# Moving the output matrices of a state-space layer behind the last attention scores

## The chip, the cores and the metric

The kernel runs on one core of a Trainium2 chip. The metric is the time of one execution on the device, in microseconds; the profile is of one such execution. The engines have separate instruction queues: TensorE (PE, with its weight loads as PEld), VectorE (DVE), ScalarE (ACT), GpSimd (POOL) and SyncE (SP), which here issues all large DMA transfers. Each works its queue in order and waits at semaphores for the others.

## What is computed

One layer of a streaming encoder over 256 frames and 16 meta tokens, width 1024: differential attention and a state-space model (S5) beside each other, an output projection, a layer norm, and a mixture of 32 experts with 4 of them for each token. Cut to what matters:

```
proj = h @ w_in                       # q, k, v (4 heads, 2 maps of 64), u (512 columns)
p = softmax(q k^T / 8 + bias)         # two maps for each head, chunk-causal
w = p[map 0] - lam * p[map 1]
att = rms_norm(w @ v)
x = scan(Abar, Bbar u);  y = Re(C x) + d * u;  ssm = glu(gelu(y))
h = layer_norm(alpha * h + [att | ssm] @ w_out)
h = layer_norm(alpha * h + moe(h))    # 32 experts, three 1024 x 1024 matrices each
```

## The kernel before

The program is written with a manual schedule: each engine's instructions run in the order of the program text. The first stage handles norm, projections, scores, states and output projection; the second streams the weights of the 32 experts through a ring of 19 chunks of 1 MB in SBUF (`ring`, `chunk`, `load_to`, issued by SP at line 551) and multiplies each with the tokens that chose it (line 1204). A chunk's place in the ring is also the place of earlier tensors: of the state tables `eb` (slot 6), the projection weights, and the matrices `AB` (slot 4), so the first chunks are issued as those are released.

The state-space model is computed in blocks of four frames. `AB` first holds the input matrices; they are transposed on TensorE into `BAT` (lines 472 to 481; odd groups are copied from PSUM by VectorE, even ones by ScalarE). `output_matrices(ri)`, for the real and the imaginary part, then makes the output matrices: `products` are three VectorE instructions over 128 x 1024 (lines 382 to 387, with `pw` as scratch), and `between_zeros` two ScalarE copies into `AB` (line 392).

Between them run four rounds, one for each head h. `states_a` are 8 products on TensorE, `states_b` nine VectorE instructions with two scans (lines 594 to 606). `scores_a(h, i)` takes the score products of the two maps in query block i (line 617), adds the bias and finds the maximum on VectorE (line 622), and takes Exp with a row sum on ScalarE (line 626). `scores_b(h, i)` inverts the sums (line 631), multiplies the second by lambda (632), scales the second map by it (633) and combines both maps (636), all on VectorE. `output_matrices(0)` stands inside round 0 between `scores_a` and `scores_b`, `output_matrices(1)` inside round 1. The k projections go to `kT` through a ScalarE copy (lines 652, 659, 667), one round ahead. `values(h)` projects v (copied by ScalarE at line 641), `value_rows(h)` transposes it (line 647, copies at 648 and 649); those of heads 0 and 1 lie in rounds 2 and 3.

After the last scores stand the lag products (lines 704 and 708), 128 small products that read both parts of `AB`; `values(2)`; `lag_b`, which copies their result (`KS`, line 719), adds the diagonal (720) and fills `ML` by eight VectorE and eight ScalarE copies (726, 728); `values(3)`; the loads of the second half of `w_out` and of the router's and bias rows; `split_w(1)`, which splits four pieces of `w_out` into a high part on ScalarE (570) and a low part on VectorE (572); `value_rows(2)` and `value_rows(3)`. Then follow the attention products (`av_a`, lines 763 to 781), the outputs of the state-space model (`out_a`, 811 and 813), the output projection (`mix`, 866 to 868), the norm, the router, and the first expert.

Of the kernel before, what the change touches and what calls it, by code (L numbers as in the profile page):

```python
# [15 lines left out]
AF = mybir.ActivationFunctionType  # L16
OP = mybir.AluOpType
# [47 lines left out]
def hybrid_layer(ctx, tc, I, out):  # L65
    nc = tc.nc
    V, S, G, T, SP = nc.vector, nc.scalar, nc.gpsimd, nc.tensor, nc.sync
# [9 lines left out]
    def nb(n=1):  # L77
        b = bank[0]
        if b + n > 8:
            b = 0  # L80
        bank[0] = (b + n) % 8
        return b

    def slot(i, shape, name, dt=F32):
        return per.tile(shape, dt, name=name, tag=f"slot{i}")
# [11 lines left out]
    def lw(shape, name, dt=F32, tag=None, bufs=None):  # L97
        return low.tile(shape, dt, name=name, tag=tag or name, bufs=bufs)
# [10 lines left out]
    def pt(shape, name, dt=F32, tag=None, bufs=None):  # L109
        return pool.tile(shape, dt, name=name, tag=tag or name, bufs=bufs)  # L110
# [74 lines left out]
    AB = slot(4, [128, 2, 16, 4, 2, 16], "AB")  # L185
# [87 lines left out]
    for db in range(8):  # L273
        if db % 2:
            S.activation(hT[:, db, :], PS[:, hb[db], :NP], AF.Identity, bias=VC[:, 8 + db:9 + db],
                         scale=VC[:, db:db + 1])
        else:
            V.tensor_scalar(hT[:, db, :], PS[:, hb[db], :NP], VC[:, db:db + 1], VC[:, 8 + db:9 + db],
                            op0=OP.mult, op1=OP.add)
# [62 lines left out]
    FW = pt([128, 2, 4, 16], "FW")  # L342
# [32 lines left out]
    def products(ri, src, tab, op, ta, tb):  # L375
        def sv(j):
            return src[:, j][:, :, None, :].to_broadcast([128, 16, 4, 16])

        def tv(j):
            return tab[:, j].rearrange("p t a -> p a t")[:, :, :, None].to_broadcast([128, 16, 4, 16])  # L380

        V.tensor_tensor(ta, sv(0), tv(ri), op=OP.mult)
        V.tensor_tensor(tb, sv(1), tv(1 - ri), op=OP.mult)
        if op == "r":
            V.tensor_tensor(ta, tb, ta, op=OP.subtract)
        else:
            V.tensor_tensor(ta, ta, tb, op=OP.add if op == "+" else OP.subtract)

    def between_zeros(dst, ri, src):
        for g2 in range(2):  # L390
            h = slice(64 * g2, 64 * g2 + 64)
            S.activation(dst[h, ri, :, :, g2], src[h], AF.Copy)

    pwf = lw([128, 1024], "pw", tag="vr")
    pw = pwf.rearrange("p (a t c) -> p a t c", a=16, t=4)
# [36 lines left out]
    CC = s8b[:, 0:512].rearrange("p (r a c) -> p r a c", r=2, a=16)  # L432
    for ri in range(2):
# [4 lines left out]
        for g2 in range(2):  # L438
            h = slice(64 * g2, 64 * g2 + 64)
            srcv = PS[h, b].rearrange("p (a g c) -> p a g c", a=16, g=2)[:, :, g2]  # L440
# [7 lines left out]
    def proj(name, fb, n0):  # L448
        b = nb()
        for kb in range(8):  # L450
            T.matmul(PS[:, b, :NP - n0], WIN[name][kb][:, fb * 128:(fb + 1) * 128], hT[:, kb, n0:],
                     start=(kb == 0), stop=(kb == 7))
        return PS[:, b, :NP - n0]
# [16 lines left out]
    BAT = [slot(f"5{c}", [128, 16, 128], "BAT") for c in "ab"]  # L470
    for ri in range(2):
        for a in range(4):
            b = nb()
            for j in range(4):
                T.transpose(PS[:, b, j * 128:(j + 1) * 128],
                            AB[:, ri, 4 * a + j].rearrange("p t g c -> p (t g c)"), ident)
            srcv = PS[:, b].rearrange("p (j c) -> p j c", j=4)
            if a % 2:
                V.tensor_copy(BAT[ri][:, 4 * a:4 * a + 4], srcv)
            else:  # L480
                S.activation(BAT[ri][:, 4 * a:4 * a + 4], srcv, AF.Copy)


    sl0 = slot("0a", [128, 2, D], "sl0")
# [3 lines left out]
    tmc = [sl0[:, j].rearrange("p (a t c) -> p a t c", a=16, t=4) for j in range(2)]  # L488

    def output_matrices(ri):  # L490
        products(ri, CC, FW, "+r"[ri], tmc[ri], pw)
        between_zeros(AB, ri, tmc[ri])

    MG = slot(1, [128, 2, 2048], "MG")
    load(MG[:, 1, :], "w_glu", 0, [[512, 128], [128 * 512, 4], [1, 512]])
# [62 lines left out]
    def load_to(n):  # L558
        while nload[0] < min(n, len(stream)):
            chunk(nload[0])  # L560
            nload[0] += 1
# [4 lines left out]
    def split_w(j, s_, l_, ks):  # L566
        if j not in W_HI:
            W_HI[j], W_LO[j] = parts4(s_, "wh", FR), parts4(l_, "wl", FR)
        for k in ks:
            S.activation(W_HI[j][k], W_OUT[j][k], AF.Copy)  # L570
        for k in ks:
            V.tensor_sub(W_LO[j][k], W_OUT[j][k], W_HI[j][k].bitcast(F32))
# [4 lines left out]
    def states_a(fb):  # L577
        vb = nb(2)
        for ri in range(2):
            for j in range(4):  # L580
                P = 4 * fb + j
                T.matmul(PS[:, vb + ri, j * 68:(j + 1) * 68], BAT[ri][:, P], u4[:, P, :], start=True, stop=True)
        VB[fb] = PS[:, vb:vb + 2, :272]
# [29 lines left out]
    def scores_a(h, i):  # L613
        nk, j0 = (144, 128) if i == 0 else (272, 0)
        sb = nb(2)
        for m in range(2):
            T.matmul(PS[:, sb + m, :nk], qT[64 * m:64 * m + 64, h, i * 128:(i + 1) * 128],
                     kT[64 * m:64 * m + 64, h, :nk], start=True, stop=True)
        s_ = sc2[:, (2 * h + i) % 2]
        mx, nm, sm_, r_ = (pt([128, 2], f"a{j}", bufs=2) for j in range(4))  # L620
        for m in range(2):
            V.tensor_tensor_reduce(s_[:, m, :nk], PS[:, sb + m, :nk], Tz[:, h, j0:j0 + nk], 1.0, -3e38,
                                   op0=OP.add, op1=OP.max, accum_out=mx[:, m:m + 1])
        V.tensor_scalar(nm, mx, -1.0, None, op0=OP.mult)
        for m in range(2):
            S.activation(s_[:, m, :nk], s_[:, m, :nk], AF.Exp, bias=nm[:, m:m + 1], accum_out=sm_[:, m:m + 1])
        SC[h, i] = s_, sm_, r_, nk

    def scores_b(h, i):
        s_, sm_, r_, nk = SC[h, i]  # L630
        V.reciprocal(r_, sm_)
        V.tensor_mul(r_[:, 1:2], r_[:, 1:2], lam)
        V.tensor_scalar(s_[:, 1, :nk], s_[:, 1, :nk], r_[:, 1:2], None, op0=OP.mult)
        w = aw[i][:, h]
        PW[h, i] = w
        V.scalar_tensor_tensor(w[:, :nk], s_[:, 0, :nk], r_[:, 0:1], s_[:, 1, :nk], op0=OP.mult, op1=OP.subtract)


    def values(h):
        vT = lw([128, NP], "vT", bufs=2)  # L640
        S.activation(vT, proj("v", h, 0), AF.Copy)
        return vT

    def value_rows(h, vT):
        b = nb()
        for blk, n in ((0, 128), (1, 128), (2, 16)):
            T.transpose(PS[:n, b, blk * 128:blk * 128 + 128], vT[:, blk * 128:blk * 128 + n], ident)
        S.activation(vr[:, 0:2, h * 128:(h + 1) * 128], PS[:, b, 0:256].rearrange("p (a e) -> p a e", a=2), AF.Copy)
        S.activation(vr[:16, 2, h * 128:(h + 1) * 128], PS[:16, b, 256:384], AF.Copy)
# [3 lines left out]
    states_b(0)  # L653
    scores_a(0, 0)
    scores_a(0, 1)
    output_matrices(0)
    states_a(1)
    scores_b(0, 0)
    S.activation(kT[:, 2, :], proj("k", 2, 0), AF.Copy)
    scores_b(0, 1)  # L660
    states_b(1)
    scores_a(1, 0)
    scores_a(1, 1)
    output_matrices(1)
    states_a(2)
    scores_b(1, 0)
    S.activation(kT[:, 3, :], proj("k", 3, 0), AF.Copy)
    scores_b(1, 1)
    states_b(2)
    vr = lw([128, 3, 512], "vr")  # L670
    vt0 = values(0)
# [12 lines left out]
    vt1 = values(1)  # L684
# [10 lines left out]
    def lt_(shape, name, tag=None, bufs=None):  # L695
        return lpool.tile(shape, F32, name=name, tag=tag or name, bufs=bufs)

    kb_ = nb()
    for fb in range(4):
        for j in range(4):  # L700
# [16 lines left out]
    def lag_b():  # L717
        KS = lt_([128, 4, 128], "KS", tag="y0")
        S.activation(KS, PS[:, kb_].rearrange("p (f c) -> p f c", f=4), AF.Copy)
        V.tensor_add(KS[:, :, 0:32], KS[:, :, 0:32], Dm)  # L720
        for j in range(4):
            for t in range(4):
                dst = ML[32 * t:32 * t + 32, :, j, 32 * t:128]
                srcv = KS[32 * j:32 * j + 32, :, 0:128 - 32 * t]
                if t < 2:
                    V.tensor_copy(dst, srcv)
                else:
                    S.activation(dst, srcv, AF.Copy)

    vt0 = values(2)  # L730
    lag_b()
    load_to(3)
    vt1 = values(3)
    wo0 = slot(3, [128, 4, D], "wo0")
    W_OUT[0] = [wo0[:, k] for k in range(4)]
    load(wo0, "w_out", 0, [[D, 128], [128 * D, 4], [1, D]])
# [6 lines left out]
    for j, n in enumerate(("b_gate", "b_up", "b_down")):  # L743
        load(bf[32 * j:32 * j + 32], n, 0, [[D, 32], [1, D]])
    split_w(1, 5, 0, (0, 1, 2, 3))
    value_rows(2, vt0)
    value_rows(3, vt1)
    load_to(5)


# [457 lines left out]
    def in_place(t, w):  # L1208
        return lambda kb: CH[place[t, w, kb // 2]][:, kb % 2]
# [227 lines left out]
    t, g, o, _, m = UNITS[u_]  # L1437
# [8 lines left out]
    def do_jobs(n):  # L1446
        for _ in range(n):
            f, *x_ = jobs.pop(0)
            f(*x_)

    r_ = linear(SI[t], 2, in_place(t, 2), transposed(ACT.pop(u_), m), m, {0: lambda: do_jobs(2), 2: lambda: do_jobs(2), 4: lambda: do_jobs(1), 6: lambda: do_jobs(1)})
# [100 lines left out]
```

## Time and profile before

| | |
|---|---|
| median of 3 runs | 1146.16 us (1142.4 to 1146.54) |
| profiled execution | 1143.38 us |
| its span, first to last instruction | 1141.6 us |
| busy: PE / DVE / ACT / POOL | 1022.5 / 365.6 / 159.6 / 106.5 us |
| DMA | 425.67 MB, mean 373 GB/s |
| mean granted TensorE clock | 0.950 |

Times in the rows are microseconds from the start of the span. A row of a timeline gives start, duration, engine, line of the program, operation, what it writes and reads, and in brackets how long its engine was idle before it and what ended that. PEclk is the granted clock of TensorE as a share of 2.4 GHz.

### The profile page before, as it was taken

The page shows a single profiled execution, that of the slowest core. Times are in us where ns is not written, and L with a number is a line of the kernel's source. Part 1 is how long each engine was busy: PE and PEld are TensorE (multiplying, and loading weights), DVE is VectorE, ACT ScalarE, POOL GpSimd, SP SyncE. Part 2 cuts the span into 40 slices and gives each one's busy share as a digit, 9 for nine tenths or more (in the row PEclk, how much of TensorE's full clock was granted, in tenths as well). Part 3 has the DMA queues.
Part 4 walks back from the last instruction along what each step waited for, and adds up shares of the span by engine and source line. Part 5 has one row for each costly group of instructions (what it writes and reads, how often), then busy time and mean ns, then how long its engine had stood idle before and what let it go on. Part 6 is the DMA issues. An engine that isn't in the chain of part 4 may idle for free. (4 is left out here: it accounts for less than half of the span.)

```text
span 1141.6 us, 16410 instructions
## 1 busy us (share of the span) xinstructions
PE 1022.5 (90%) x6572; PEld 527.3 (46%) x6572; DVE 365.6 (32%) x755; ACT 159.6 (14%) x329; POOL 106.5 (9%) x223
## 2 busy tenths in 40 slices
PE   6986997899999788997999977799999999998665
PEld 5865884344554344445444433344453444453222
DVE  7999664222122212321131221122222212222103
ACT  1734423000010000111001000010000000001000
POOL 2300004101100110021001010101101010010001
PEclk9999897999999989998999988999999999999779
DMA  7824286999999999999999999999999999999894
GB/s 220 288 96 167 94 341 253 385 375 420 421 421 421 421 420 420 422 420 421 421 421 420 420 421 420 421 421 421 421 421 421 421 421 394 423 419 420 329 419 195
DMA packets 72313, 425.67 MB, mean 373 GB/s; under 512 B 14925, under 2 KB 15546, under 8 KB 23210
## 3 DMA queue, kind: packets, MB, share of 16 engines
q1 hardware_dynamic: 72234, 424.58, 91.3%
q8 instruction: 53, 0.87, 0.3%
q14 instruction: 26, 0.21, 0.1%
HBM read 423.50 MB, written 1.87 MB: 373 GB/s over the span
## 5 line engine op out<-in xcount | busy, mean ns | idle before, releaser
L1204 PE MATMUL PS<-wx,xgp 128*32 128x256 f32 (+2 forms) x3008 | 484.3, 492 | 38.8 <-DMA wx<-in_w_gate 19.5
L1204 PEld LDWEIGHTS PS<-wx,xgp 128*32 128x32 f32 (+2 forms) x3008 | 185.0, 133 | 296.4 <-issue 203.0
L1204 PE MATMUL PS<-wx,yT 128*32 128x256 f32 (+2 forms) x1504 | 231.0, 473 | 8.8 <-DMA wx<-in_w_down 8.0
L1204 PEld LDWEIGHTS PS<-wx,yT 128*32 128x32 f32 (+2 forms) x1504 | 91.5, 129 | 133.6 <-issue 93.4
L946 POOL COPY si<-P 96x32 bf16<-96x32 bf16 (+2 forms) x32 | 7.4, 233 | 754.8 <-PE PS L1198 724.9
L1251 DVE COPY yc<-PS 32x256 f32<-32x256 f32 (+1 forms) x39 | 20.0, 514 | 159.6 <-ACT yc L1253 159.6
L1157 PEld LDWEIGHTS PS<-ohp,hr 128*128 128x128 f32 x512 | 65.8, 206 | 9.6 <-issue 9.6
L1157 PE MATMUL PS<-ohp,hr 128*128 128x128 f32 x512 | 68.1, 294 | 0.2 <-DVE ohp L1149 0.2
L1226 DVE TENSOR_SCALAR PS<-PS 128x256 f32<-128x256 f32 (+2 forms) x33 | 22.6, 684 | 123.4 <-PE PS L1204 123.4
L1198 PE MATMUL PS<-B,si 96*32 96x256 bf16 (+2 forms) x282 | 40.4, 340 | 16.7 <-SPq L1307 9.7
L1220 DVE TENSOR_SCALAR g<-PS 128x256 f32<-128x256 f32 (+1 forms) x27 | 14.9, 553 | 114.4 <-PE PS L1204 100.6
L1253 ACT ACTIVATE yc<-PS 32x256 f32<-32x256 f32 (+1 forms) x39 | 17.4, 446 | 239.0 <-PE PS L1204 232.7
L1237 DVE COPY yT<-PS 128x512 f32<-128x512 f32 (+1 forms) x39 | 22.7, 594 | 85.6 <-PE PS L1236 85.6
L1288 DVE SCALAR_TENSOR_TENSOR lo<-yc,gc,hi 128x1024 fp32r<-128x1024 f32 x15 | 19.3, 1285 | 86.7 <-ACT hi L1287 85.5
L1302 DVE TENSOR_TENSOR acc<-PS,acc 128x1024 f32<-128x1024 f32 x30 | 35.4, 1220 | 16.6 <-PE PS L1299 16.4
L1161 ACT ACTIVATE xgp<-PS 128x512 f32<-128x512 f32 x16 | 9.6, 598 | 216.4 <-PE PS L1157 216.4
L1198 PEld LDWEIGHTS <-si 96*32 96x32 bf16 (+2 forms) x282 | 11.5, 102 | 50.3 <-issue 47.8
L1147 POOL TENSOR_SCALAR gop<-io,PMs,Gs 128x32 f32<-128x32 f32 (+2 forms) x60 | 33.1, 565 | 0.0
L1221 ACT ACTIVATE PS<-g 128x256 f32<-128x256 f32 (+1 forms) x27 | 13.2, 491 | 138.4 <-DVE g L1220 138.4
L1220 DVE TENSOR_SCALAR yc<-PS 128x1024 f32<-128x1024 f32 x6 | 7.3, 1225 | 78.4 <-PE PS L1204 78.4
L1299 PE MATMUL PS<-hi,gt 128*128 128x512 f32 x60 | 26.6, 443 | 3.0 <-ACTq L1307 3.0
L1299 PE MATMUL PS<-lo,gt 128*128 128x512 f32 x60 | 25.1, 419 | 0.7 <-DVE lo L1288 0.7
(389 smaller groups left out, 845.9 us busy)
## 6 DMA issues: line engine op xcount, KB each, us to landing
wx<-in_w_gate SPq DMA_DIRECT2D x128, 1024.0 KB, 19.8
wx<-in_w_up SPq DMA_DIRECT2D x128, 1024.0 KB, 19.8
wx<-in_w_down SPq DMA_DIRECT2D x127, 1024.0 KB, 19.7
w_u<-in_w_in SPq DMA_DIRECT2D x2, 1024.0 KB
w_q<-in_w_in SPq DMA_DIRECT2D x1, 2048.0 KB
w_k<-in_w_in SPq DMA_DIRECT2D x2, 1024.0 KB
w_v<-in_w_in SPq DMA_DIRECT2D x1, 2048.0 KB
wo<-in_w_out SPq DMA_DIRECT2D x2, 1024.0 KB
```

Source lines behind the costliest of these rows:

```text
L1147: eng.tensor_scalar(dst[:, i, o:o + m], iv, pc, gg[:, i, t:t + 1], op0=OP.is_equal, op1=OP.mult)
L1157: T.matmul(PS[:, 4 + h, k * 128:k * 128 + n], hr[:, i, rows_of(db)], oh_[:, i, :n], start=(i == 0), stop=(i == 1))
L1198: T.matmul(o, sel[:, :m], B96[:, w, f * n:f * n + n], start=True, stop=False)
L1204: T.matmul(PS[(f % nf) * m:(f % nf) * m + m, b + f // nf, :n], xT(kb), c[:, f * n:f * n + n], start=False, stop=(kb == 7))
L1220: V.tensor_scalar(g_, r_, 7.0, None, op0=OP.min)
L1226: V.tensor_scalar(r_, r_, 7.0, -7.0, op0=OP.min, op1=OP.max)
L1237: V.tensor_copy(yT[:, 4 * a:4 * a + nk], PS[:, b, :nk * 128].rearrange("p (k s) -> p k s", k=nk))
L1251: V.tensor_copy(d_, s_)
L1253: S.activation(d_, s_, AF.Copy)
L1288: V.scalar_tensor_tensor(lo[:n], YC[g][:n], GC[g][:n], hi[:n].bitcast(F32), op0=OP.mult, op1=OP.subtract)
L1299: T.matmul(PS[:, 4 + 2 * i + h], GT[g][:n, i * 128:(i + 1) * 128], part[:n, h * 512:(h + 1) * 512], start=(j == 0), stop=(j == 1))
L1302: V.tensor_tensor(acc[:, i].rearrange("p (h c) -> p h c", h=2), PS[:, 4 + 2 * i:6 + 2 * i], acc[:, i].rearrange("p (h c) -> p h c", h=2), ...
```

## The change

Four edits. All eight copies of `BAT` are made by ScalarE. The scaling of the second map in `scores_b` is done by ScalarE, with the factor as a per-partition scale. `output_matrices` is no longer in rounds 0 and 1: its products stand behind the last `scores_b`, each set ahead of one of the projections `values(2)` and `values(3)`, which come forward, and each `between_zeros` behind the projection that follows its products. The products use a new scratch tile, `pw2`, in the place of the score buffers (tag "as"). `value_rows(2)` and `value_rows(3)` come forward with them; the lag products, `lag_b` and `split_w(1)` follow after all of these.

```diff
--- before.py
+++ after.py
@@ -475,10 +475,7 @@
                 T.transpose(PS[:, b, j * 128:(j + 1) * 128],
                             AB[:, ri, 4 * a + j].rearrange("p t g c -> p (t g c)"), ident)
             srcv = PS[:, b].rearrange("p (j c) -> p j c", j=4)
-            if a % 2:
-                V.tensor_copy(BAT[ri][:, 4 * a:4 * a + 4], srcv)
-            else:
-                S.activation(BAT[ri][:, 4 * a:4 * a + 4], srcv, AF.Copy)
+            S.activation(BAT[ri][:, 4 * a:4 * a + 4], srcv, AF.Copy)
 
 
     sl0 = slot("0a", [128, 2, D], "sl0")
@@ -488,8 +485,7 @@
     tmc = [sl0[:, j].rearrange("p (a t c) -> p a t c", a=16, t=4) for j in range(2)]
 
     def output_matrices(ri):
-        products(ri, CC, FW, "+r"[ri], tmc[ri], pw)
-        between_zeros(AB, ri, tmc[ri])
+        products(ri, CC, FW, "+r"[ri], tmc[ri], pw2)
 
     MG = slot(1, [128, 2, 2048], "MG")
     load(MG[:, 1, :], "w_glu", 0, [[512, 128], [128 * 512, 4], [1, 512]])
@@ -630,7 +626,7 @@
         s_, sm_, r_, nk = SC[h, i]
         V.reciprocal(r_, sm_)
         V.tensor_mul(r_[:, 1:2], r_[:, 1:2], lam)
-        V.tensor_scalar(s_[:, 1, :nk], s_[:, 1, :nk], r_[:, 1:2], None, op0=OP.mult)
+        S.activation(s_[:, 1, :nk], s_[:, 1, :nk], AF.Copy, scale=r_[:, 1:2])
         w = aw[i][:, h]
         PW[h, i] = w
         V.scalar_tensor_tensor(w[:, :nk], s_[:, 0, :nk], r_[:, 0:1], s_[:, 1, :nk], op0=OP.mult, op1=OP.subtract)
@@ -653,7 +649,6 @@
     states_b(0)
     scores_a(0, 0)
     scores_a(0, 1)
-    output_matrices(0)
     states_a(1)
     scores_b(0, 0)
     S.activation(kT[:, 2, :], proj("k", 2, 0), AF.Copy)
@@ -661,7 +656,6 @@
     states_b(1)
     scores_a(1, 0)
     scores_a(1, 1)
-    output_matrices(1)
     states_a(2)
     scores_b(1, 0)
     S.activation(kT[:, 3, :], proj("k", 3, 0), AF.Copy)
@@ -695,6 +689,15 @@
     def lt_(shape, name, tag=None, bufs=None):
         return lpool.tile(shape, F32, name=name, tag=tag or name, bufs=bufs)
 
+    pw2 = lw([128, 1024], "pw2", tag="as").rearrange("p (a t c) -> p a t c", a=16, t=4)
+    output_matrices(0)
+    vt0 = values(2)
+    between_zeros(AB, 0, tmc[0])
+    output_matrices(1)
+    vt1 = values(3)
+    value_rows(2, vt0)
+    between_zeros(AB, 1, tmc[1])
+    value_rows(3, vt1)
     kb_ = nb()
     for fb in range(4):
         for j in range(4):
@@ -727,10 +730,8 @@
                 else:
                     S.activation(dst, srcv, AF.Copy)
 
-    vt0 = values(2)
     lag_b()
     load_to(3)
-    vt1 = values(3)
     wo0 = slot(3, [128, 4, D], "wo0")
     W_OUT[0] = [wo0[:, k] for k in range(4)]
     load(wo0, "w_out", 0, [[D, 128], [128 * D, 4], [1, D]])
@@ -743,8 +744,6 @@
     for j, n in enumerate(("b_gate", "b_up", "b_down")):
         load(bf[32 * j:32 * j + 32], n, 0, [[D, 32], [1, D]])
     split_w(1, 5, 0, (0, 1, 2, 3))
-    value_rows(2, vt0)
-    value_rows(3, vt1)
     load_to(5)
```

## Rows read from the trace of the kernel before

**Rows 1.** Stages: us, busy time (x count) by engine, PEclk, DMA share, GB/s.

```profile
180.00:190.00 10.00, 6.80 (x38) 5.06 (x37) 6.71 (x33) 3.34 (x7) 6.06 (x3) 0.67 0.44 182
...
260.00:280.00 20.00, 19.41 (x194) 8.79 (x192) 7.37 (x10) 2.13 (x3) 2.35 (x5) 1.00 1.01 420
```

**Rows 2.** Weight queue in order of time: start, us, issue, count.

```profile
97.43 0.82 SPq L551 DMA_DIRECT2D wx<-in_w_gate  x2
...
171.74 22.09 SPq L551 DMA_DIRECT2D wx<-in_w_down  x4
```

**Rows 3.** VectorE in order of time, rounds 0 and 1: start, us, instruction.

```profile
53.93 2.48 DVE L479 COPY BAT<-PS 128x512 f32<-128x512 f32 x4
57.10 0.72 DVE L594 TENSOR_TENSOR s8b<-PS,eb 128x544 f32<-128x544 f32 x1 [0.69 <-PE PS L582]
...
62.67 0.30 DVE L622 CUSTOM_DVE_ANT_0 as<-PS,Tz 128x144 f32<-128x144 f32 x1
...
64.24 1.22 DVE L382 TENSOR_TENSOR sl<-s8b,FW 128x1024 f32<-128x1024 f32 x1
...
67.77 0.16 DVE L631 RECIPROCAL a<-a 128x2 f32<-128x2 f32 x1
...
68.15 0.29 DVE L633 TENSOR_SCALAR as<-as,a 128x144 f32<-128x144 f32 x1
...
69.97 0.72 DVE L594 TENSOR_TENSOR s8b<-PS,eb 128x544 f32<-128x544 f32 x1
```

**Rows 4.** VectorE in order of time, last round and split.

```profile
98.10 0.30 DVE L622 CUSTOM_DVE_ANT_0 as<-PS,Tz 128x144 f32<-128x144 f32 x1
...
102.21 0.72 DVE L713 COPY m<-ident 32x32 f32<-32x32 f32 x4
...
108.62 4.63 DVE L572 TENSOR_TENSOR wl<-wo,wh 128x1024 fp32r<-128x1024 f32 x4 [1.33 <-ACT wh L570]
113.17 0.27 DVE L766 COPY wT<-PS 16x128 f32<-16x128 f32 x1
```

**Rows 5.** ScalarE in order of time, first and last round.

```profile
63.45 0.41 ACT L626 ACTIVATE as<-as,a 128x144 f32<-128x144 f32 x1 [2.31 <-DVE a L624]
...
64.36 0.52 ACT L626 ACTIVATE as<-as,a 128x272 f32<-128x272 f32 x1
...
65.30 0.19 ACT L626 ACTIVATION_READ_ACCUMULATOR as<-as,a 128x1 f32 x1
67.88 2.12 ACT L392 ACTIVATE AB<-sl 64x1024 f32<-64x1024 f32 x2 [2.40 <-DVE sl L387]
...
101.30 0.37 ACT L641 ACTIVATE vT<-PS 128x272 f32<-128x272 f32 x1
101.58 0.57 ACT L719 ACTIVATE KS<-PS 128x512 f32<-128x512 f32 x1
104.13 2.96 ACT L728 ACTIVATE MG<-KS 32x256 f32<-32x256 f32 x8 [1.99 <-issue]
...
107.53 3.90 ACT L570 ACTIVATE wh<-wo 128x1024 fp32r<-128x1024 f32 x4
```

**Rows 6.** TensorE in order of time: start, us, instruction, idle before and releaser.

```profile
63.38 3.88 PE L451 MATMUL PS<-hT,w_k 128*128 128x272 f32 x16
...
94.02 0.28 PE L704 MATMUL PS<-s8a 128*32 128x32 f32 x4 [1.44 <-DVE s8b L595]
...
96.44 0.50 PE L708 MATMUL PS<-AB,s8a 128*32 128x96 f32 x6
...
119.20 0.69 PE L811 MATMUL PS<-MG,u 128*64 128x128 f32 x2
```

**Rows 7.** TensorE in stretches of 2 us: us, busy (x count), PEclk, DMA share, GB/s.

```profile
110.00:112.00 2.00, 0.00 (x0) 0.54 1.07 356
112.00:114.00 2.00, 1.29 (x4) 0.50 0.95 203
...
124.00:126.00 2.00, 2.00 (x21) 1.00 0.00 0
```

## The prediction

> **What bounds the kernel now.** I read the table of stages first. From about 260 us to the overflow code near 1050 the DMA engines are busy the whole time at about 420 GB/s [rows 1]: expert weights stream in, and what remains of them fixes the time from there. The question is what starts that stream. Between 180 and 190 us the DMA share falls to 0.44 [rows 1], and the weight queue shows why: the four down chunks of the first position take 22.09 us to be issued, from 171.74 on [rows 2], because the ring of 19 chunks is full and nobody has consumed chunk 0 yet. So the transfers have slack just before the experts start, and the start of the first expert product (about 191 us) sets everything behind it: ring full, then consumption, then a saturated queue. A step that reaches that start later moves the end one for one.
>
> What reaches it is a serial chain of attention and state-space work. In order of views: VectorE from 57 to 104 us [rows 3, 4], which has next to no gap, then ScalarE [rows 5], then TensorE [rows 6]. The points to see are: VectorE finishes the last score at 102.21 (the next row is the mask copy) [rows 4]; ScalarE ends its half of the lag copies and begins to split the output weights at 107.53 [rows 5]; VectorE's low halves follow at 108.62, and only behind them stands the copy at 113.17 that the first attention product needs [rows 4]. From there the order is unchanged down to the first expert. I therefore ask one thing: when does split_w(1) begin on ScalarE, 107.53 now [rows 5]?
>
> **The change, part by part.**
>
> The copies of the BAT transposes. VectorE's four took 2.48 us from 53.93, but its next operation waited 0.69 us for TensorE anyway and began at 57.10 [rows 3]. Nothing is gained there. On ScalarE eight copies now follow each other; the fifth is what the first state product needs, about when TensorE gets to it. I take zero, at most 0.4 us lost; the cover is TensorE's own transposes.
>
> The scores without products. A round, from its first biased score to the next round's state work, took 62.67 to 69.97 = 7.30 us, of which the three products took 64.24 to 67.77 = 3.53 us [rows 3]. Rounds 0 and 1 have this form; rounds 2 and 3 have no products and took 98.10 to 102.21 = 4.11 us [rows 4]. Taking the products out frees 2 x 3.53 = 7.06 us of VectorE, and the scaling frees eight instructions of 0.29 us or a little more [rows 3].
>
> The scaling on ScalarE. The nearest row to it is the Exp with a per-partition operand: 0.41 us for 144 columns, 0.52 for 272, against 0.29 on VectorE for 144 [rows 3, 5]. The lower bound is a plain copy, 0.37 for 272 [rows 5]; I take the Exp, since it too reads SBUF and a per-partition operand. The Trainium skill, "ScalarE: Activation LUTs", section "Rules for kernel authors", sends a multiplication to VectorE and not to ScalarE; the rows above agree in direction. Its section "What ACT_TABLE_LOAD costs" gives 186 ns + 0.833 ns a column, and 93 ns for each pointer operand, an estimate of 0.40 and 0.51 us here; the sum would be the same within 0.1 us.
>
> The duration is the small part. The scale stands in ScalarE's queue behind all four Exps of the round, and in rounds 2 and 3 behind two value-row copies too, and VectorE then waits for it with everything of the next round queued behind. Round 0: ScalarE is through with the Exps at 65.30 + 0.19 = 65.49 [rows 5]; scale to about 65.8, combination on VectorE, reciprocal and lambda product; but before the second scale stands the copy of the third k projection, which TensorE ends at 63.38 + 3.88 = 67.26 [rows 6]. Copy to 67.6, scale to 68.1, combination: next state work at about 68.6, where it was 69.97. Gain 1.4 us. Round 1 has the same form with its projection ready earlier: 2.8 (Exps) + 0.4 + 0.45 + 0.4 + 0.55 + 0.45, about 5.0 us for 7.30. Gain 2.3. Rounds 2 and 3: ScalarE comes free 101.30 - 98.10 = 3.20 us into the round [rows 4, 5] (the row at 101.30 is the first behind the value rows); then scale 0.41, combination 0.46, reciprocal and product 0.4, scale 0.52, combination 0.48: 5.47 us instead of 4.11. Loss 1.36 each. Together 1.4 + 2.3 - 2.7 = 1.0: the last score ends at about 101.2, not at 102.21, although some 9.9 us of VectorE's work were taken away ahead of it.
>
> What is put behind it. Two sets of products, 2 x 3.53 = 7.06, end at 108.3. The first between_zeros lies beside the second set. The second does not: 2.12 us on ScalarE [rows 5] to about 110.5. Only then can the lag products run, for they read both halves of AB, and TensorE takes them in written order. The value projections on TensorE take the bank wait that the lag products had (1.44 us [rows 6]) and are done around 100 us; they hide nothing of this, being finished before the matrices are begun. The lag products took 94.02 to 96.94 = 2.9 us [rows 6] and lay beside the last round; they are now bare.
>
> Their clock is the unknown. TensorE would have had almost nothing for ten us before them. In the trace, after a shorter pause from 105 us on, the granted clock fell: 0.54 in 110 to 112 with no busy time, 0.50 in 112 to 114 [rows 7], the 1.2 GHz level. So the lag products take 2.9 us at 2.4 GHz and up to 5.8 at 1.2. The Trainium skill, "TensorE: Matmul & The Clock Gate", section "What's actually happening", says that the engine goes to 1.2 GHz after idling and that sustained work brings 2.4 back; the trace agrees (0.50 and 1.00), and by it the upper end is the likelier.
>
> Then the KS copy of 0.57 us [rows 5], the addition of the diagonal and the hops between engines, together about 1.0 us, and ScalarE's lag copies, 2.96 us [rows 5], before split_w(1). So split_w(1) starts at 110.5 + 2.9 + 1.0 + 3.0 = 117.4 with a fast clock and about 120.3 with a slow one: **10 to 13 us later** than 107.53. I take 11.5. On ScalarE the last value-row copies no longer stand between the split and the attention weights (under a us), but VectorE's 113.17 ends later than those, so nothing comes back.
>
> The DMAs. The state buffers' release lets chunks 1 and 2 start about 2 us before 97.43 [rows 2], and the second half of the output weights starts earlier by some us behind the value projections. Nobody waits for these. The bias rows now wait for the product scratch (same buffer), at about 108 us; they are needed only by the bias split beside the mixing products. The chunks behind them wait for split_w(0) and the mixing products, which are in the chain and go later with it. At the end the ring is full before the first expert as now.
>
> **The sum.** The profiled execution took 1143.38 us (span 1141.6 and 1.8 around it): 1143.4 + 11.5 = 1154.9. The median of the runs is 2.8 above it, which would give 1157.7. I say 1156.
>
> **Rivals.**
> First, that it is not slower: VectorE keeps running because ScalarE is ready in time for each scale. Then the last score ends 9.9 us sooner, at about 92.3 (TensorE's scores permit it), the matrices lie beside the value projections, and split_w(1) starts at 92.3 + 7.1 + 2.2 + 2.9 + 1.0 + 3.0 = 108.5, 1.0 us late, 3.9 with a slow clock: 1144.4 to 1147.3 by the profiled execution, up to 1150 by the median. It decides if ScalarE reaches the scale within about 2 us of a round's begin. Against it stand the four Exps, 63.45 to 65.49 [rows 5], all ahead of it in the queue. Chance 0.10.
>
> Second, that the stream and not the chain sets the end. Then only the release of the state buffers counts, 2 us sooner: 1141.4, by the median 1144. For it speaks the saturated queue from 260 us on [rows 1]; against it the 22.09 us of a full ring [rows 2]. Chance 0.06.
>
> Third, that the lag products wake the clock for what follows: the attention and first output products then run at 2.4 GHz where they had 1.2 until 124 us [rows 7]. VectorE's copies pace the attention products; the outputs begin at 119.20 [rows 6], so some 4.8 us of them lie at the low clock, and would save half, about 2. Then the shift is 8 us: 1151 to 1154. Slower still. Chance 0.14.
>
> **How the numbers follow.** The forecast (10 to 13 us later) has 0.70. A measurement of this kernel tells about 0.5% (5.7 us) from no change: the runs themselves reach from 1142.4 to 1146.54. The forecast and the third rival are slower by more than that but for unlucky medians (0.04): 0.80. The first rival and most of the second are within: with those medians 0.17. Faster has 0.03, the part of the second in which w_v's release counts as well. The range goes from 1148, which cuts into the first rival, to 1161: the median with 13 us, and 2 us for its spread.
>
> **What would show it.** Right: VectorE idle ahead of the second operation of every scores_b, released by ScalarE's scale; the first state rows of round 1 near 68.6; products behind 101 us; lag products starting near 110.5 with a granted clock near 0.5; split_w(1) at 117 to 120; the first expert product later by the same amount, and 420 GB/s behind it. Wrong: the last score before 95 us; lag products before 104; a first expert product at its old time; or a DMA share near 1 just ahead of the first expert.

## The result and the profile after

The changed kernel took 1155.16 us in the median of 4 runs (1153.92 to 1157.6), the kernel before 1145.02 in the 4 runs that now stand beside it: a ratio of 1.0092, 95% interval 1.007 to 1.0114, so about 10 us slower. The profiled execution took 1155.1 us with a span of 1153.3.

VectorE of the changed kernel in order of time shows the four rounds and what now follows them. The brackets give the idle time ahead of a row and what ended it; [rows 3, 4] are the same work before.

```profile
58.06 0.72 DVE L590 TENSOR_TENSOR s8b<-PS,eb 128x544 f32<-128x544 f32 x1 [3.87 <-PE PS L578]
...
63.64 0.30 DVE L618 CUSTOM_DVE_ANT_0 as<-PS,Tz 128x144 f32<-128x144 f32 x1
...
66.78 0.37 DVE L632 SCALAR_TENSOR_TENSOR aw<-as,a 128x144 f32<-128x144 f32 x1 [1.07 <-ACT as L629]
...
69.11 0.50 DVE L632 SCALAR_TENSOR_TENSOR aw<-as,a 128x272 f32<-128x272 f32 x1 [1.68 <-ACT as L629]
69.52 0.72 DVE L590 TENSOR_TENSOR s8b<-PS,eb 128x544 f32<-128x544 f32 x1
...
75.09 0.30 DVE L618 CUSTOM_DVE_ANT_0 as<-PS,Tz 128x144 f32<-128x144 f32 x1
...
79.95 0.72 DVE L590 TENSOR_TENSOR s8b<-PS,eb 128x544 f32<-128x544 f32 x1
...
85.52 0.30 DVE L618 CUSTOM_DVE_ANT_0 as<-PS,Tz 128x144 f32<-128x144 f32 x1
...
90.80 0.72 DVE L590 TENSOR_TENSOR s8b<-PS,eb 128x544 f32<-128x544 f32 x1
...
96.37 0.30 DVE L618 CUSTOM_DVE_ANT_0 as<-PS,Tz 128x144 f32<-128x144 f32 x1
...
101.22 0.50 DVE L632 SCALAR_TENSOR_TENSOR aw<-as,a 128x272 f32<-128x272 f32 x1 [0.65 <-ACT as L629]
101.64 1.22 DVE L382 TENSOR_TENSOR sl<-s8b,FW 128x1024 f32<-128x1024 f32 x1
...
108.70 0.72 DVE L716 COPY m<-ident 32x32 f32<-32x32 f32 x4
...
115.56 0.29 DVE L723 TENSOR_TENSOR KS<-KS,Dm 128x128 f32<-128x128 f32 x1 [5.42 <-ACT KS L722]
```

A round's biased scores begin at 63.64, 75.09, 85.52 and 96.37; the rows beginning at 69.52, 79.95, 90.80 and 101.64 are the work behind them. The rounds thus take 5.88, 4.86, 5.28 and 5.27 us. The combination at 66.78 waited 1.07 us for ScalarE, that at 69.11 1.68, the last, at 101.22, 0.65. The products stand bare from 101.64 to 108.70 (TensorE's value projections had ended at 99.80); VectorE's next wait is one of 5.42 us for KS.

The longest waits of VectorE between 57 and 102 us, changed kernel (who waited, for whom, us in total, times, longest):

```profile
DVE aw L632 <- ACT as L629: 8.8, 8, 1.7
DVE s8b L590 <- PE PS L578: 3.9, 1, 3.9
```

The kernel before has only one entry in the same stretch, 0.7 us for TensorE at its beginning. The 3.9 us here are the time in which VectorE used to copy BAT: the work went away and left a wait, and the state work begins no sooner. The 8.8 us are the eight scales. Five of these waits, 1.07 to 1.68 us each, come from what stands ahead of the scale in ScalarE's queue: the Exps, a k projection's copy, value rows. The other three are of 0.65 us each; there ScalarE was free and itself waited for VectorE's lambda product, so that what VectorE waits for is the scale and the hand-over there and back.

ScalarE of the changed kernel; [rows 5] answers to it.

```profile
99.51 0.40 ACT L629 ACTIVATE as<-as,a 128x144 f32<-128x144 f32 x1
100.67 0.52 ACT L629 ACTIVATE as<-as,a 128x272 f32<-128x272 f32 x1 [0.77 <-DVE a L628]
...
108.82 2.12 ACT L392 ACTIVATE AB<-sl 64x1024 f32<-64x1024 f32 x2 [0.57 <-DVE sl L385]
...
114.93 0.60 ACT L722 ACTIVATE KS<-PS 128x512 f32<-128x512 f32 x1 [3.43 <-PE PS L711]
115.93 2.96 ACT L731 ACTIVATE MG<-KS 32x256 f32<-32x256 f32 x8 [0.41 <-DVE KS L723]
118.91 3.90 ACT L566 ACTIVATE wh<-wo 128x1024 fp32r<-128x1024 f32 x4
```

The second map's scale at 99.51 follows the value-row copies without a gap: it was queued, not late. The one at 100.67 is of the other kind. The second between_zeros ends at 110.94, KS starts at 114.93, the split of the output weights at 118.91.

TensorE of the changed kernel, lag products and first outputs, and its granted clock in stretches of 2 us (busy time, clock, DMA share, GB/s); [rows 6, 7] answer to them.

```profile
110.99 0.37 PE L711 MATMUL PS<-AB,s8a 128*32 128x96 f32 x1 [1.53 <-ACT AB L392]
...
114.39 0.50 PE L711 MATMUL PS<-AB,s8a 128*32 128x96 f32 x6
...
130.58 0.69 PE L810 MATMUL PS<-MG,u 128*64 128x128 f32 x2
```

```profile
112.00:114.00 2.00, 2.00 (x76) 0.50 0.19 53
114.00:116.00 2.00, 1.48 (x39) 0.99 0.00 0
...
118.00:120.00 2.00, 0.00 (x0) 0.50 0.00 0
...
130.00:132.00 2.00, 2.00 (x9) 0.50 0.04 8
```

The first few lag products run ahead; the bulk begins at 110.99, after a wait of 1.53 us for the second half of AB, and ends at 114.89. The clock was at 0.50 for most of them and rose near 114; it fell again ahead of the first outputs, which began at 0.50 as they did before. The first expert product stands at 201.37; it stood at 191.00 in the kernel before. The weight queue still spends 21.58 us on the four chunks that find the ring full:

```profile
182.79 21.58 SPq L547 DMA_DIRECT2D wx<-in_w_down  x4
```

### The profile page after: what moved, and what is told of

The parts are those of the page before. It is cut to its first block, busy times and chain, and to the rows that moved or that the text cites. A ratio compares the mean times of both kernels' runs of the same rounds, so it can differ in the third digit from the quotient of the medians.

```text
span 1153.3 us, 16408 instructions
## 1 busy us (share of the span) xinstructions
PE 1028.8 (89%) x6572; PEld 527.3 (46%) x6572; DVE 360.6 (31%) x743; ACT 164.9 (14%) x341; POOL 106.6 (9%) x223
## 5 line engine op out<-in xcount | busy, mean ns | idle before, releaser
L1203 PE MATMUL PS<-wx,yT 128*32 128x256 f32 (+2 forms) x1504 | 232.5, 476 | 10.1 <-DMA wx<-in_w_down 9.2
L1197 PEld LDWEIGHTS <-si 96*32 96x32 bf16 (+2 forms) x282 | 11.5, 103 | 50.2 <-issue 47.9
L1244 ACT ACTIVATE yc<-PS 128x1024 f32<-128x1024 f32 x6 | 6.1, 1025 | 138.0 <-PE PS L1203 138.0
```

Of the source, the lines that this page charges most:

```text
L1197: T.matmul(o, sel[:, :m], B96[:, w, f * n:f * n + n], start=True, stop=False)
L1203: T.matmul(PS[(f % nf) * m:(f % nf) * m + m, b + f // nf, :n], xT(kb), c[:, f * n:f * n + n], start=False, stop=(kb == 7))
```

## Experiments

To compare runs, two points of each trace were read: the start of split_w(1) on ScalarE and the first expert product on TensorE. The executions differ by up to 1.7 us before any edited instruction is reached, so both are taken from a common point ahead of the edits, the second between_zeros of the input matrices (48.52 us in the kernel before, 49.49 in the changed one). The split then begins 59.01 us behind that point in the kernel before, the first expert 142.48 us behind it. The table gives the shifts against these. A trace is of a single execution, and the executions of one kernel end up to 9 us apart (of e3_move's ten, six took 1148.98 to 1150.22 us and four 1155.05 to 1157.92); those traced of e2_scale, e5_split_late and e9_warm were the shortest of their kernel, that of e11_split_late_again the second shortest. In the expectations, chain theory means that the end moves one for one with the start of split_w(1).

| kernel | split_w(1) | first expert | ratio of times, 95% interval |
|---|---|---|---|
| changed kernel | +10.4 | +9.4 | 1.0092 (1.007 to 1.0114) |
| e1_bat | 0.0 | -0.9 | 1.0003 (0.9981 to 1.0025) |
| e2_scale | +6.7 | +5.5 | 1.0061 (1.0042 to 1.0079) |
| e3_move | +5.9 | +5.8 | 1.0061 (1.0036 to 1.0085) |
| e4_pool | 0.0 | 0.0 | 1.002 (1.0 to 1.004) |
| e5_split_late | moved | -4.2 | 0.9989 (0.9971 to 1.0006) |
| e6_split_halves | moved | +1.4 | 1.0035 (1.0019 to 1.0051) |
| e7_chunks_late | 0.0 | +0.2 | 0.9997 (0.9982 to 1.0011) |
| e8_split_rows | moved | -2.2 | 0.9979 (0.9957 to 1.0001) |
| e9_warm | +9.3 | +9.3 | 1.0108 (1.0083 to 1.0133) |
| e10_split_warm | moved | -0.6 | 1.0045 (1.0031 to 1.0058) |
| e11_split_late_again | moved | -4.9 | 1.0002 (0.9984 to 1.002) |

**The BAT copies alone.**

```diff
-            if a % 2:
-                V.tensor_copy(BAT[ri][:, 4 * a:4 * a + 4], srcv)
-            else:
-                S.activation(BAT[ri][:, 4 * a:4 * a + 4], srcv, AF.Copy)
+            S.activation(BAT[ri][:, 4 * a:4 * a + 4], srcv, AF.Copy)
```

> The kernel before with the BAT copies alone given to ScalarE. Chain theory: 0 us; VectorE's first state operation waits for TensorE's state products at 57 us with or without these copies. Rival (VectorE's work sets the stretch wherever it is taken from): 2.5 us faster.

1145.46 us beside 1144.66, and no shift at the split. 2.5 us of VectorE's work taken away ahead of a wait for TensorE are worth nothing.

**The scale alone.**

```diff
-        V.tensor_scalar(s_[:, 1, :nk], s_[:, 1, :nk], r_[:, 1:2], None, op0=OP.mult)
+        S.activation(s_[:, 1, :nk], s_[:, 1, :nk], AF.Copy, scale=r_[:, 1:2])
```

> The kernel before with the scaling of the second map alone given to ScalarE. Chain theory: rounds 2 and 3 lose 1.36 us each behind the Exps and value rows, and in rounds 0 and 1 the scale now stands behind between_zeros too (2.12 us, which ends 2.3 us after the reciprocal), so each of them loses about 2.2: 7 us later at split_w(1) and at the end. Rival (the wait for ScalarE is hidden, the move of the products alone cost the time): 0, or 3 us faster by VectorE's freed work.

1152.12 us beside 1144.66. ScalarE and VectorE of round 0 in this run:

```profile
68.11 2.12 ACT L392 ACTIVATE AB<-sl 64x1024 f32<-64x1024 f32 x2 [2.40 <-DVE sl L387]
70.26 0.41 ACT L633 ACTIVATE as<-as,a 128x144 f32<-128x144 f32 x1
```

```profile
70.71 0.37 DVE L636 SCALAR_TENSOR_TENSOR aw<-as,a 128x144 f32<-128x144 f32 x1 [2.36 <-ACT as L633]
```

The scale at 70.26 stands right behind between_zeros, which waited for the products and then ran 2.12 us; the combination waited 2.36 us for it, and the next round's state work begins at 72.41. The edit takes 2.6 us of instructions off VectorE, and costs 6.7. VectorE's eight waits for the scale add up to 10.3 us. Four of them, 7.7 us together, are for the first scale of a round, which stands in the queue behind between_zeros or behind the Exps and the value rows; the other four, of 0.65 us each, find ScalarE free. So the place in ScalarE's queue costs most, the hand-over the rest; the scale's own 0.40 and 0.52 us, for 0.29 and 0.36 on VectorE, is the small part.

**The move alone.** The changed kernel with the two edits above undone.

> The changed kernel with scaling and BAT copies as before: only the move is left. Chain theory: the last score ends about 7 us sooner (95.5), but products (7.1), the second between_zeros (2.2), the lag products at 1.2 GHz (4), KS and lag copies (4) follow bare, so split_w(1) starts at 112 to 114, 5 to 6.5 us later than 107.5, and the end moves by as much. Rival (only the scaling cost time, the move hides beside the value projections): 0 to 7 us faster.

1150.17 us beside 1144.66; the split 5.9 us late. Without the scale on ScalarE, VectorE waits 0.7 us in the whole stretch from 57 to 102, as in the kernel before, and the last score ends near 95.7, 6.5 us sooner than [rows 4] has it. All of that and 5.9 us more go to what now stands behind it:

```profile
99.31 2.12 ACT L392 ACTIVATE AB<-sl 64x1024 f32<-64x1024 f32 x2 [4.19 <-DVE sl L387]
...
102.84 2.12 ACT L392 ACTIVATE AB<-sl 64x1024 f32<-64x1024 f32 x2 [0.57 <-DVE sl L385]
...
109.29 0.60 ACT L725 ACTIVATE KS<-PS 128x512 f32<-128x512 f32 x1 [3.77 <-PE PS L714]
...
113.28 3.90 ACT L569 ACTIVATE wh<-wo 128x1024 fp32r<-128x1024 f32 x4
```

Between 99.31 and 113.28 there are two between_zeros, a wait of 3.77 us for the bare lag products, KS and the lag copies, where the kernel before had the last round. So both edits cost time, and together less than their sum (10.4 for 6.7 + 5.9), since with the move no between_zeros stands ahead of the scales in rounds 0 and 1.

**The weight stream.** The calls load_to(3) and load_to(5) taken out of the kernel before, so that chunks 1 to 4 go out with load_to(7).

> The kernel before without the two calls that issue chunks 1 to 4 at 97 and 131 us, so that they go out with chunks 5 and 6 at 139 us: 4 MB, or 10 us of transfers at 420 GB/s, moved behind that point. Chain theory: the full ring had that much slack (no transfer for some 8 us before the experts, and gaps before), so 0 to 1 us. Rival (the weight stream sets the end): about 10 us slower.

1144.77 us beside 1144.71. The weight queue of this run ([rows 2] before; this trace lies 1.57 us later at the common point):

```profile
113.56 1.93 SPq L551 DMA_DIRECT2D wx<-in_w_gate  x2
...
133.29 0.33 SPq L551 DMA_DIRECT2D wx<-in_w_gate  x1
...
173.48 22.20 SPq L551 DMA_DIRECT2D wx<-in_w_down  x4
```

The edit moved less than the expectation says. SyncE went on to the calls of load_to(7) as soon as it had issued what stands ahead of them: chunks 1 and 2 went out at 113.56, some 15 us late, and the next one at 133.29 for 131.54, no later than before. So 2 MB, about 5 us of transfers at 420 GB/s, were late by 15 us, and that changes nothing: the queue still stands 22.20 us before a full ring. The rival in which the stream sets the end is out for delays of this size, and so is the idea that releasing the state buffers 2 us sooner could have paid.

**The products on another engine.** The kernel before with the six products on GpSimd, early, and the copies into AB behind the scores of round 1 and the value rows of round 2.

```diff
-        V.tensor_tensor(ta, sv(0), tv(ri), op=OP.mult)
+        eng.tensor_tensor(ta, sv(0), tv(ri), op=OP.mult)      # eng = G for the output matrices
...
+    output_matrices(0)          # behind the memset of MG, products only
+    output_matrices(1)
```

> The kernel before with the six products of the output matrices on GpSimd, early, and the between_zeros copies later in ScalarE's queue; scaling and BAT copies as before. Chain theory: VectorE loses 7.06 us ahead of the last score and the lag products still lie beside the last round, so split_w(1) starts about 6.5 us sooner (101) and the end moves by as much. Rival 1 (the weight stream sets the end): 0 to 2 us faster. Rival 2 (GpSimd's work slows VectorE's or comes too late for ScalarE): no gain or a loss.

1147.36 us beside 1144.66, and the split where it was. The third part of the expectation, VectorE slowed by GpSimd, is what happened. GpSimd and VectorE in the same stretch:

```profile
60.24 2.22 POOL L382 TENSOR_TENSOR sl<-s8b,FW 128x1024 f32<-128x1024 f32 x1
```

```profile
58.28 0.72 DVE L595 TENSOR_TENSOR s8b<-PS,eb 128x544 f32<-128x544 f32 x1
...
59.66 0.91 DVE L597 TENSOR_TENSOR s8b<-s8b 128x272 f32<-128x272 f32 x1
60.50 2.26 DVE L598 TENSOR_TENSOR s8b<-s8b 128x272 f32<-128x272 f32 x1
62.68 5.27 DVE L600 TENSOR_TENSOR_SCAN sw<-eb,s8b 128x272 f32<-128x272 f32 x2
```

Two scans that take 1.33 us in the changed kernel's round took 5.27 here, and the two operations ahead of them 0.91 and 2.26 where 0.44 and 0.43 are usual. VectorE lost what it had been spared. The Trainium skill, "SBUF — State Buffer", section "Who interferes with whom", says that a VectorE instruction with two SBUF inputs contends with a GpSimd instruction that reads SBUF, over a port pair that the two engines share. The trace agrees: the operation at 58.28, which reads PSUM and one SBUF tile, kept its 0.72 us, and those that read two SBUF tiles were stretched.

**Shortening the chain at the same place.** If the start of split_w(1) is what counts, taking split_w(1) off the way to the attention product must pay. It was moved behind av_b(0), whole and then in halves, ahead of the part of split_w(0) that reuses its tiles.

```diff
-    split_w(1, 5, 0, (0, 1, 2, 3))
...
     av_b(0)
+    split_w(1, 5, 0, (0, 1, 2, 3))
     split_w(0, 8, 2, (0, 1))
```

> The kernel before with split_w(1) moved behind av_b(0), ahead of the first half of split_w(0), which reuses its tiles. Chain theory: VectorE reaches the first attention copy 4.6 us sooner (its four low halves are out of the way) and ScalarE 3.9; behind av_b(0) VectorE's gaps take in some 3 us of the split, so the first expert starts about 3 us sooner and the end is at -3 us. Rival (split_w(1) only happened to stand there and something else, the value projections or the weight stream, holds the attention): 0.

> As the run before it, but split_w(1) in halves, each ahead of the half of split_w(0) that reuses its tile. Chain theory: 2 to 4 us sooner; which of the two is better depends on where VectorE's gaps lie. Rival: 0.

The whole split moved brings the first expert 4.2 us forward (its start at 186.72, for 191.00): the chain theory holds at that point. But the time is 1144.23 us beside 1144.71, a ratio whose interval takes in 1. In halves, four low-half operations, 4.81 us together, stand between the two pairs of attention copies of the second query block, and the first expert comes 1.4 us later; the time is 1148.6 us. The whole move was repeated:

> The kernel before with split_w(1) behind av_b(0), once more and with more rounds, since three rounds left its end open (0.997 to 1.0006) though the first expert started 4.3 us sooner. Chain theory one for one: -4 us. If shifts of a few us are lost in the expert stage: -1 us.

1145.43 us beside 1144.65, 1.0002: the first expert is 4.9 us sooner and nothing of it can be seen in the median, although the lowest of its runs (1139.23) lies below every run of the kernel before. By the median the second form of the expectation fits better. The traced executions themselves did end sooner, with spans of 1138.1 us (e5_split_late) and 1138.2 for 1141.6, and took 951.4 and 952.1 us from the first expert to the end, as the others do. So the gain reached the end there; the longer executions left no trace, and where they lose it stays open.

**VectorE or TensorE as the pace of the first attention product.** As the move of the whole split, and the eight residual-row operations (5.6 us) taken out of that product.

> As the first run of this group, and the eight residual-row operations (5.6 us of VectorE) are taken out of the first attention product too and put four behind the second and four behind the bias split. Chain theory: VectorE paces the first attention product, so the outputs start some 4 us sooner again: 5 to 7 us faster than the kernel before. Rival (TensorE at 1.2 GHz paces the attention product): no more than the first run of this group.

The outputs began no sooner than in e5_split_late (115.04 here, 114.31 there). A row of e5_split_late and one of this run, then TensorE from 110 to 112 us in the same order (busy time, clock, DMA share, GB/s):

```profile
110.67 0.48 PE L780 MATMUL PS<-vr,wT 16*128 16x128 f32 x2 [0.46 <-DVE wT L765]
110.79 0.28 ACT L764 ACTIVATE wT<-PS 128x128 f32<-128x128 f32 x1 [1.84 <-PE PS L762]
```

```profile
110.00:112.00 2.00, 1.29 (x8) 1.00 1.01 412
110.00:112.00 2.00, 2.00 (x8) 0.50 1.08 339
```

In e5_split_late VectorE had no gap from 109.00 on and TensorE waited for its copies: there the rows did set the pace. Here VectorE's copies waited for ScalarE's, those 1.84 and 1.49 us for TensorE's transposes, and TensorE was busy throughout at a clock of 0.50, where e5_split_late had 1.00. So TensorE at the low clock has taken over as the pace, as the rival says. Why the clock fell sooner here was not tried, and what the rows are worth at the full clock is not shown. 1142.05 us, a ratio of 0.9979 (0.9957 to 1.0001): not clear of no change.

**The clock.** The changed kernel with 104 transposes whose result nothing reads.

```diff
+    def dummies(n):
+        for _ in range(n):
+            T.transpose(PS[:, kb_, 0:128], ident, ident)
+    dummies(36)
     value_rows(3, vt1)
+    dummies(16)
...
+            if i == 0 and h == 1:
+                dummies(52)
```

> The changed kernel with 104 idle transposes added on TensorE, none of which anything reads: 36 ahead of the last value rows, 16 ahead of the lag products, 52 ahead of the first attention product's waits, so that its clock stays at 2.4 GHz from 100 us to the first outputs. Third rival of the prediction, and chain theory: the lag products take 2.9 us instead of 3.9, the first outputs begin at 2.4 GHz instead of 1.2 (some 2 us), so the first expert starts 2 to 3 us sooner than in the changed kernel and the end is 7 to 8 us behind the kernel before instead of 10. If the clock has no part in the shift: 10 us, as the changed kernel.

TensorE in stretches of 4 us (busy time, clock, DMA share, GB/s), this run:

```profile
108.00:112.00 4.00, 3.60 (x120) 1.00 0.47 113
...
124.00:128.00 4.00, 4.00 (x14) 0.50 0.00 0
```

The clock is 1.00 through the lag products, which now take from 109.97 to 112.77, 2.8 us for 3.9, and the split begins 1.1 us sooner than in the changed kernel. But the last transposes end near 119.4, the attention product's gaps follow, and from 124 on the clock is down again: the first outputs begin at 0.50 as before. The end shows nothing of the 1.1 us (1154.42 us, 1.0108). So the clock's part in the lateness of the split is about 1 us, of which the first expert (+9.3 for +9.4) and the end show nothing, and whether warm outputs would have given back the 2 us of the third rival is not decided, since they were not warm.

The same with the split moved and 46 transposes in the kernel before:

> The kernel before with split_w(1) moved behind av_b(0), and 46 idle transposes on TensorE in the waits ahead of the first outputs, where the trace of that move alone showed 0.50 and 0.68 from 114 to 118 us. Chain theory: the first outputs run about 1.3 us shorter, the first expert starts 4 to 5.5 us sooner than in the kernel before, and the end is at -2 to -5 us. If shifts of a few us are lost in the expert stage: within 0.2% of the kernel before.

1149.47 us beside 1144.65, slower. The transposes got in the way of the attention product (ScalarE's last copy of its weights waited 3.66 us for TensorE, where e5_split_late's longest such wait was 1.25), the first outputs still ran at 0.50, now nearly all of the first group of four, and the first expert came 4 us later than with the move alone. And there is a second loss, which e6_split_halves has too. From the first expert to the end of the span it is 950.4 to 952.1 us in the kernel before, the changed one and every other run, but 954.9 in e6_split_halves and 956.7 in e10_split_warm. Stretches from 36 us ahead of the end on, of the kernel before and of e10_split_warm, 4 us each (busy time, clock, DMA share, GB/s):

```profile
1105.60:1109.60 4.00, 3.62 (x30) 0.50 1.02 428
1109.60:1113.60 4.00, 3.46 (x36) 0.50 1.01 416
...
1117.60:1121.60 4.00, 3.14 (x21) 1.00 1.00 415
```

```profile
1120.00:1124.00 4.00, 3.15 (x13) 0.50 1.00 413
1124.00:1128.00 4.00, 4.00 (x19) 0.50 0.56 216
```

In both, the clock falls while the last weights come in. In the kernel before it is at 0.50 from 36 to 28 us ahead of the end and at 1.00 behind that; in e10_split_warm the low stretch lies 8 us later against the end, from 28 to 20 us, with TensorE busy throughout (4.00) as the last transfers end. The first and the last of the same groups of products, in the kernel before and in e10_split_warm:

```profile
1118.46 1.98 PE L1402 MATMUL PS<-acc,ident 128*128 128x512 f32 x4 [1.16 <-DVE yc L1251]
...
1129.02 3.72 PE L1457 MATMUL PS<-g,yc 128*128 128x256 f32 x16 [0.55 <-DVE g L1454]
```

```profile
1121.91 3.78 PE L1409 MATMUL PS<-acc,ident 128*128 128x512 f32 x4 [0.85 <-DVE yc L1258]
...
1135.39 3.72 PE L1464 MATMUL PS<-g,yc 128*128 128x256 f32 x16 [0.55 <-DVE g L1461]
```

From the start of the one to the start of the other TensorE has no gap but the last 0.55 us, and it takes 10.56 us in the kernel before and 13.48 in e10_split_warm. In e6_split_halves it takes 13.46, with the first group at 3.78 and the low stretch at the same distance from the end. So 2.9 us of the 4.3 us that e6_split_halves has more than the kernel before, and of the 6.1 of e10_split_warm, are work done at 0.50 that had been done at 1.00. The other 1.4 and 3.1 us were lost between the first expert and there, and their cause is not shown. Why the drop lies where it lies was not tried.

## Why the prediction came out right

**The place.** The forecast rested on one point, the start of split_w(1), and on one for one behind it. The changed kernel's split came 10.4 us late (10 to 13 forecast, 11.5 taken), its first expert 9.4, its end 10.1. e2_scale and e3_move, at +6.7 and +5.9, show the same: about 7 us each at the end, by ratio. e7_chunks_late shows that 2 MB going out 15 us later change nothing, so the transfers had room. One for one is shown to a microsecond or two, for shifts of 6 us and more, in the direction of slower; for e9_warm's 1.1 us it is not, and for e5_split_late's 4 us in the other direction only in the traced executions, not in the median.

**The scores.** Round by round, from [rows 3, 4] and ScalarE's queue: forecast 5.9, 5.0, 5.5 and 5.5 us, measured 5.88, 4.86, 5.28 and 5.27. Last score at 101.2 forecast, at 101.64 on a trace that was 0.97 late ahead of the edits, so 100.7. The last score came 0.5 us sooner than forecast. The step that mattered, that ScalarE reaches the scale only behind the Exps and the value rows, is what the waits show: 8.8 us in eight. ScalarE took up the first scale 2.7 to 3.1 us into a round (99.51 for 96.37 in the last), where the first rival needed about 2. The hand-over, 0.65 us even where ScalarE was free, stands in the forecast only inside the sums of the rounds.

**What stands behind.** Products 7.06 us forecast and measured (101.64 to 108.70); second between_zeros to 110.5 forecast, 110.94 measured (110.0 without the 0.97); KS and addition 1.0, measured 1.0; lag copies 2.96, measured 2.96.

**The clock.** This was the one term with wide bounds, 2.9 to 5.8 us, and I leaned to the upper one. It measured 3.9 for the bulk: the clock was low, as forecast, but a few products had run ahead and the clock came back during the rest. The 11.5 us held about 4.5 for it, 0.6 too much; that is about half of the 1.1 us by which the split was put too late. The other half is the scores. The third rival (the lag products wake the clock for the outputs) did not happen: the clock was up at 114 to 116 and down at 118 again.

**The rest.** BAT at zero: e1_bat. Nothing lost to the DMAs: the first chunks went out at 95.70, 1.7 us sooner than [rows 2] (2.7 from the common point), for nobody. The offset from the profiled execution to the median, which I had at 2.8, was 1.6 with the fourth run and 0.1 in the changed kernel. The sum with that offset was 1157.7, and 1156 was put in its place without a reason; that it came out only 0.8 us above the time is luck. The shift itself was put 1.4 us too large at the end (11.5 for 10.1).

## What to carry to other kernels

An instruction handed to a less busy engine starts when that engine's queue reaches it: write down what stands ahead of it there, and what stands behind the one that waits, before counting the work that is taken away. Even where the queue is free, the hand-over there and back is a wait, here 0.65 us for an instruction of 0.36. Work moved from a busy place to a later one is hidden only if the engines are still busy with something that does not need it; here the projections that should have covered it were done before it could begin. Where a chain leads to a stage that is bound by its stream, find the one start that passes a delay on, and measure every edit there: in the end time, shifts of 4 us were lost in a spread of 4 to 9 us between executions of the same kernel.

## What the runs showed that was not expected

GpSimd's product beside VectorE stretched single VectorE operations up to fivefold (0.43 us in the kernel before, 2.26 here) and two scans from 1.33 to 5.27 us, so the idle GpSimd was no free place for products of two SBUF tensors. And the time from first expert to end is not the same constant for every edit ahead of it: two runs had 4 to 6 us more, both with some of the last products in a stretch of low clock, which accounts for 2.9 us in each. No kernel here is faster than the kernel before beyond its interval.
